# Moving token sums ahead of their splits, and two residual additions behind, in the last projection of a two-layer trunk

## The chip, the core and the metric

The kernel runs on one NeuronCore of a Trainium2 chip. The metric is the device time of one execution, in microseconds (us). Five engines work side by side, each through its own list of instructions in order, and wait for each other by semaphores: TensorE (PE in the profile; PEld is its weight load) multiplies matrices into banks of PSUM, VectorE (DVE) and ScalarE (ACT) do elementwise work, GpSimd (POOL) and SyncE (SP) here mostly issue DMA transfers.

## The reference

The model has two layers and a last norm. The second layer is multi-head latent attention; the change lies in its output projection, the last matrix product of the program:

```python
def mla_layer(x, cos, sin, norm_g, w_in, q_norm_g, w_q_b, kv_norm_g, w_kv_b, w_out):
    ...
    o = causal_mla_attention(q_nope, q_rope, k_nope, k_rope, v)
    y = o.reshape(B, S, MLA_WIDTH) * jax.nn.silu(z)
    return x + y @ w_out          # y: 512 x 2048, w_out: 2048 x 1024

def reference(...):
    ...
    return rmsnorm(x, final_norm)  # 512 x 1024, float32
```

`y` is 512 tokens by 2048 channels, `w_out` 2048 by 1024, `x` is the residual, all in float32.

## The kernel before

**Three matmuls for one.** A float32 operand is split into a high part and the rest: ScalarE writes `hi` (line 188 for tokens, 559 for weights), VectorE subtracts and writes `lo` (line 189, 560). `mm3` then multiplies hi by hi, lo by hi and hi by lo (lines 183, 184, 185) into the same bank. Each line of the profile with 183 to 185 is one of those three.

**Seven products for eight.** The projection is cut in two by tokens, by channels and by output columns, and is done by seven half-size products in the manner of Strassen, on sums of token blocks (`a11`, `a12`, `a21`, `a22`, all pieces of the tile `y`, stored with channels on the partitions) and on sums of weight blocks. VectorE makes the token sums (`combine_rows`, line 1055, two 128-channel rows at a time, 512 columns per instruction). `split_rows` cuts four rows at a time (1024 columns per instruction) into one of two token buffers, `slots[0]` and `slots[1]`, each with a `hi` and a `lo`. The weight sums are made by the DMA itself: SyncE loads a block (line 548), GpSimd issues a load that adds onto it (line 546). There are two such sets of weight tiles, `x_sum` (named `b_x`, four loads of 256 KB a strip) and `y_sum` (named `b_y`, two loads of 512 KB a strip).

**Strips and banks.** A product is `multiply(banks, strips, slot, start)`: two strips of weights of four rows each (`q` = 0, 1), and for each strip two token tiles (`t` = 0, 1) in two PSUM banks; four parts of 12 matmuls, 48 in all. A strip has a `hi` and a `lo` buffer from a ring of four (`WB = 4`), so there is room for two strips: strip `q` of a product can be split only when TensorE is done with strip `q` of the product before. With `start=False` the product adds onto what the banks hold. `gather` (line 610) is the addition of a bank to the residual `xs`, on VectorE, 512 columns; a product that goes on in that bank has to wait for it.

**What sets the order.** The tail is written in `products` and `finish` under a manual schedule: every engine does its share in the order in which it is written there. The first product runs inside the last heads of the attention; then follow

1. second: banks `both`, strips `t1` of `x_sum`, `slots[0]`
2. third: banks `last`, strips `p2` of `y_sum`, `slots[1]` (tokens `a12`)
3. fourth: banks `both`, strips `y1` of `y_sum`, `slots[0]` (tokens `n3 = s2 + a12`, written over `a12`)
4. fifth: banks `acc`, strips `t2` of `x_sum`, `slots[1]` (tokens `s2`)
5. sixth: banks `acc`, strips `y2` of `y_sum`, `slots[0]`
6. seventh, in `finish`, with the last norm and the stores.

Between the fourth and the fifth stand also `square` (ScalarE, line 1219: sums of squares of the residual for the last norm) and `total` (GpSimd).

Of the kernel before, what the change touches and what calls it, by code (L numbers as in the profile page):

```python
# [15 lines left out]
ALU = mybir.AluOpType  # L16
# [34 lines left out]
def trunk_kernel(  # L51
# [41 lines left out]
    def bank(dtype=F32):  # L93
        return ps.tile([P, 512], dtype, name="bank", tag="bank")
# [92 lines left out]
    def halves(src, hi, lo):  # L187
        act.activation(hi, src, AF.Copy)  # L188
        dve.tensor_tensor(lo, src, f32(hi), ALU.subtract)
# [51 lines left out]
    def start():  # L241
# [85 lines left out]
        for k in range(4):  # L327
            ready(0, k)
            products(0, k)
        w_lo(0, 4, 2)  # L330
        w_lo(1, 4, 2)
        ready(0, 4)
        products(0, 4)
        square(2)
        power(2)
        ready(0, 5)
        products(0, 5)
        ready(0, 6)
        scale(2)
# [194 lines left out]
    LEFT, RIGHT = slice(0, 512), slice(512, D)  # L534
# [35 lines left out]
    def quarters():  # L570

        return [
            [
                y[:, half * 8 + 2 * i : half * 8 + 2 * i + 2, t * 256 : (t + 1) * 256]
                for i in range(4)
            ]
            for t in range(2)
            for half in range(2)
        ]
# [21 lines left out]
    def multiply(banks, strips, slot, start, then=None):  # L601
        for q in range(2):
            for t in range(2):
                part(banks[t], strips[q], slot, q, t, start and q == 0, q == 1, not start)
                if then and q == 1:
                    then(t)

    def gather(t, c, b, op=ALU.add):

        dve.tensor_tensor(xs[:, t, c], xs[:, t, c], b, op)  # L610


    a11, a12, a21, a22 = quarters()

    slots = [tuple(v[:, :, s * 256 : (s + 1) * 256] for v in (h_hi, h_lo)) for s in range(2)]
# [7 lines left out]
    x_sum, y_sum = Summed(w_out, 2), Summed(w_out, 2)  # L623
# [7 lines left out]
    acc = [bank() for _ in range(2)]  # L631
# [399 lines left out]
    def values(h):  # L1031
# [17 lines left out]
    a11, a12, a21, a22 = (  # L1049
        y[:, half * 8 : half * 8 + 8, t * 256 : (t + 1) * 256] for t in range(2) for half in range(2)  # L1050
    )

    def combine_rows(out, a, b, op, k0, k1):
        for k in range(k0, k1, 2):
            dve.tensor_tensor(*(v[:, k : k + 2, :] for v in (out, a, b)), op)  # L1055

    def split_rows(src, slot, k0, k1):
        halves(*(v[:, k0:k1, :] for v in (src, *slot)))
    x_sum, y_sum = Summed(w_out2, 1), Summed(w_out2, 2)
# [38 lines left out]
    first_half, slots = {}, {}  # L1098
    for h in range(H):
        p, odd = divmod(h, 2)  # L1100
        g, t = divmod(h + 5, 4)
        if h == 12:
# [3 lines left out]
            acc = [bank() for _ in range(2)]  # L1106
# [47 lines left out]
    s3, s2 = a21, a11  # L1154
# [5 lines left out]
    def products():  # L1160

        combine_rows(s1, a21, a22, ALU.subtract, 6, 8)
        split_rows(s1, slots[0], 6, 8)
        x_sum.load(1, RIGHT, add=True, pieces=range(4))
        t1.append(x_sum.strip(1))
        x_sum.load(1, RIGHT, add=True, pieces=range(4, 8))
        multiply(both, t1, slots[0], True)
        split_rows(a12, slots[1], 0, 4)
        p2 = [y_sum.strip(0)]
        split_rows(a12, slots[1], 4, 8)  # L1170
        combine_rows(s3, a11, a21, ALU.subtract, 6, 8)
        combine_rows(s2, s1, a11, ALU.subtract, 6, 8)
        for t in range(2):
            gather(t, LEFT, acc[t])
        p2.append(y_sum.strip(1))
        y_sum.load(1, RIGHT)
        multiply(last, p2, slots[1], True)
        n3 = a12
        combine_rows(n3, s2, a12, ALU.add, 0, 4)
        split_rows(n3, slots[0], 0, 4)  # L1180
        combine_rows(n3, s2, a12, ALU.add, 4, 8)
        split_rows(n3, slots[0], 4, 8)
        for t in range(2):
            gather(2 + t, RIGHT, both[t])
        y1 = y_sum.strips()
        y_sum.load(0, RIGHT, add=True)
        multiply(both, y1, slots[0], False)
        split_rows(s2, slots[1], 0, 4)
        split_rows(s2, slots[1], 4, 8)
        for t in range(2):  # L1190
            gather(t, LEFT, last[t])
            square(t, LEFT)
            total(t)
        t2 = x_sum.strips()
        x_sum.load(1, LEFT, add=True)
        multiply(acc, t2, slots[1], False)
        split_rows(s3, slots[0], 0, 4)
        split_rows(s3, slots[0], 4, 8)
        for t in range(2):
            gather(t, RIGHT, both[t])  # L1200
        y2 = [y_sum.strip(0)]
        for t in range(2):
            gather(t, RIGHT, acc[t], ALU.subtract)
        y2.append(y_sum.strip(1))
        for t in range(2):
            square(t, RIGHT)
            power(t)
        multiply(acc, y2, slots[0], False)
        split_rows(a22, slots[1], 0, 4)
        split_rows(a22, slots[1], 4, 8)  # L1210
# [6 lines left out]
    def square(t, c):  # L1217
        r = sm.tile([P, 1], F32, name="ssq", tag="ssq8", bufs=12)
        act.activation(
            junk[:, : c.stop - c.start], xs[:, t, c], AF.Square, scale=D**-0.5, accum_out=r  # L1220
        )
        ssq[t].append(r)

    def total(t):

        r = sm.tile([P, 1], F32, name="total")
        pool.tensor_scalar(r, ssq[t][0], EPS, None, ALU.add)
        for q in ssq[t][1:]:
            pool.tensor_tensor(r, r, q, ALU.add)
        ssq[t] = [r]  # L1230

    def power(t):

        rs[t] = sm.tile([P, 1], F32, name="rs")
        pool.tensor_tensor(rs[t], ssq[t][1], ssq[t][0], ALU.add)
        pool.tensor_tensor(rs[t], rs[t], mhalf, ALU.pow)
# [92 lines left out]
```

## Time and profile before

| | us |
|---|---|
| median of three runs | 718.78 |
| lowest, highest | 718.22, 719.83 |
| the profiled execution, its own time | 719.61 |
| its span, first to last instruction | 717.8 |
| TensorE busy | 701.5 |
| VectorE busy | 444.5 |
| ScalarE busy | 347.2 |

The span is what the rows of the trace fill; the execution's own time is 1.81 us longer than its span. Times in rows count from the span's start. A row of the timeline gives start, duration, engine, line, operation, output and inputs with their sizes, a count where equal instructions follow each other, and in brackets the idle time before it with the instruction that the profile takes to have ended it. Where a row stands for several instructions, its duration covers all of them; consecutive ones overlap slightly, so that the pitch (start to start) is a little shorter than the duration of one.

### The profile page before, as it was taken

The numbers are of one execution on the slowest core, as the hardware profiler recorded it, in microseconds if no ns is written. First come the engines' busy times: TensorE is split into PE (matmuls) and PEld (weight loads), VectorE is DVE, ScalarE is ACT, GpSimd is POOL, SyncE is SP. The second block draws the span as 40 slices with busy tenths as digits, with TensorE's granted clock in tenths as the row PEclk, the third lists the DMA queues.
The fourth block names the chain that finished last, engine by engine and source line by source line (L and its number), as shares of the span: only waits on it lengthen the run. The fifth ranks groups of instructions, "written<-read, shape, count | busy, mean of one in ns | idle before, by whom it ended". The sixth has DMA issues, their size and how long they took to land.

```text
span 717.8 us, 10049 instructions
## 1 busy us (share of the span) xinstructions
PE 701.5 (98%) x3529; PEld 600.8 (84%) x3529; DVE 444.5 (62%) x866; ACT 347.2 (48%) x748; POOL 138.0 (19%) x182
## 2 busy tenths in 40 slices
PE   6999999999999999999999999999999999998996
PEld 6988888888888888799888888898899889986785
DVE  5963452562586897751644211686776787798775
ACT  6452332241343565554642324755575575655553
POOL 5000000000001341154600006221232131031621
PEclk9999999999999999999999999999999999999899
DMA  7342332333355997233432524113132265287843
GB/s 250 113 145 69 117 91 86 105 90 100 101 155 135 236 195 124 89 110 107 125 115 73 140 74 125 53 45 89 53 95 59 73 164 136 44 202 176 156 79 118
DMA packets 69475, 82.79 MB, mean 115 GB/s; under 512 B 12080, under 2 KB 45872, under 8 KB 69424
## 3 DMA queue, kind: packets, MB, share of 16 engines
q1 hardware_dynamic: 60384, 65.10, 30.2%
q0 software_dynamic: 8896, 16.78, 13.7%
q8 instruction: 28, 0.46, 0.3%
q10 hardware_dynamic: 144, 0.26, 0.1%
q14 instruction: 23, 0.19, 0.1%
HBM read 75.83 MB, written 2.10 MB: 109 GB/s over the span
## 4 chain that ended last, share of the span: by engine, by line
PE 93%; DVE 3%; issue 1%; ACT 1%; DMA 0%; POOL 0%; POOLq 0%; SPq 0%; DVEq 0%; ACTq 0%
PE bank L184 28%; PE bank L183 28%; PE bank L185 28%; PE bank L1022 2%; PE bank L301 2%; PE bank L986 1%; PE bank L985 1%; DVE w_lo L560 1%; DVE y L1055 1%; PE bank L226 1%; PE bank L1044 0%; PE bank L988 0%; DVE xs L610 0%; DMA xs<-in_x 0%; ACT a_hi L188 0%
## 5 line engine op out<-in xcount | busy, mean ns | idle before, releaser
L166 ACT ACTIVATE w_hi<-raw 128x512 fp32r<-128x512 f32 (+2 forms) x192 | 100.2, 576 | 134.3 <-PE bank L184 121.2
L167 DVE TENSOR_TENSOR w_lo<-raw,w_hi 128x512 fp32r<-128x512 f32 x124 | 81.6, 691 | 114.7 <-ACT w_hi L166 114.0
L183 PE MATMUL bank<-h_hi,w_hi 128*128 128x512 f32 x368 | 143.5, 390 | 0.0
L185 PE MATMUL bank<-h_lo,w_hi 128*128 128x512 f32 x368 | 143.3, 389 | 0.0
L184 PE MATMUL bank<-h_hi,w_lo 128*128 128x512 f32 x368 | 143.3, 389 | 0.0
L167 POOL TENSOR_TENSOR w_lo<-raw,w_hi 128x256 fp32r<-128x256 f32 (+2 forms) x68 | 61.3, 927 | 175.4 <-ACT w_hi L166 174.5
L185 PEld LDWEIGHTS bank<-h_lo,w_hi 128*128 128x128 f32 x368 | 69.1, 188 | 14.4
L184 PEld LDWEIGHTS bank<-h_hi,w_lo 128*128 128x128 f32 x368 | 69.1, 188 | 14.2
L183 PEld LDWEIGHTS bank<-h_hi,w_hi 128*128 128x128 f32 x368 | 69.1, 188 | 14.2
L183 PE MATMUL bank<-w_hi,h_hi 128*128 128x512 f32 (+1 forms) x176 | 64.6, 367 | 0.0
L184 PE MATMUL bank<-w_hi,h_lo 128*128 128x512 f32 (+1 forms) x176 | 64.2, 364 | 0.0
L185 PE MATMUL bank<-w_lo,h_hi 128*128 128x512 f32 (+1 forms) x176 | 64.1, 364 | 0.0
L183 PE MATMUL bank<-w_hi,a_hi 128*128 128x512 f32 (+1 forms) x116 | 45.9, 395 | 2.5 <-ACT w_hi L559 2.5
L185 PE MATMUL bank<-w_lo,a_hi 128*128 128x512 f32 (+1 forms) x116 | 45.6, 393 | 0.5 <-DVE w_lo L560 0.5
L184 PE MATMUL bank<-w_hi,a_lo 128*128 128x512 f32 (+1 forms) x116 | 45.6, 393 | 0.0
L183 PE MATMUL bank<-latT_hi,w_hi 128*128 128x512 f32 x104 | 42.4, 408 | 0.0
L184 PE MATMUL bank<-latT_hi,w_lo 128*128 128x512 f32 x104 | 40.6, 391 | 0.0
L185 PE MATMUL bank<-latT_lo,w_hi 128*128 128x512 f32 x104 | 40.6, 390 | 0.0
L559 ACT ACTIVATE w_hi<-b_x 128x512 fp32r<-128x512 f32 (+1 forms) x40 | 29.8, 796 | 20.9 <-PE bank L184 10.3
L560 DVE TENSOR_TENSOR w_lo<-b_x,w_hi 128x512 fp32r<-128x512 f32 (+1 forms) x40 | 34.0, 900 | 9.4 <-ACT w_hi L559 9.3
L183 PEld LDWEIGHTS bank<-w_hi,h_hi 128*128 128x128 f32 x176 | 33.1, 188 | 4.4
L185 PEld LDWEIGHTS bank<-w_lo,h_hi 128*128 128x128 f32 x176 | 33.1, 188 | 4.4
(204 smaller groups left out, 1404.8 us busy)
## 6 DMA issues: line engine op xcount, KB each, us to landing
raw<-in_pool_w_in SPq DMA_DIRECT2D x64, 256.0 KB, 3.0
raw<-in_mla_w_in SPq DMA_DIRECT2D x32, 256.0 KB, 3.1
b_x<-in_pool_w_out POOLq DMA_DIRECT2D x12, 512.0 KB, 7.6
b_x<-in_mla_w_out POOLq DMA_DIRECT2D x24, 256.0 KB, 6.5
raw<-in_mla_w_q_b SPq DMA_DIRECT2D x36, 128.0 KB, 2.3
raw<-in_pool_w_group SPq DMA_DIRECT2D x16, 256.0 KB, 2.7
q_r<-stack SPq DMA_DIRECT2D x64, 64.0 KB, 2.0
raw<-in_mla_w_kv_b SPq DMA_DIRECT2D x16, 256.0 KB, 3.0
```

What stands on the lines that cost most here:

```text
L166: act.activation(hi, raw, AF.Copy)
L167: ins = eng.tensor_tensor(lo, raw, f32(hi), ALU.subtract)
L183: pe.matmul(o, a[0], b[0], start=start, stop=False, skip_group_check=more)
L184: pe.matmul(o, a[1], b[0], start=False, stop=False, skip_group_check=more)
L185: pe.matmul(o, a[0], b[1], start=False, stop=stop, skip_group_check=more)
L226: pe.transpose(pt[:, i * P : (i + 1) * P], xn[:, k * P : (k + 1) * P], ident)
L301: pe.matmul(first[i][:, c], w0.views[0][a][:, k, i * P : (i + 1) * P], (h_hi, h_lo)[b][:, k, c], start=k == 0 and n == 0, stop=k == KD - 1 ...
L559: act.activation(hv[:, k, :], raw, AF.Copy)
L560: eng.tensor_tensor(lv[:, k, :], raw, f32(hv[:, k, :]), ALU.subtract)
L985: pe.matmul(o, q_r[h // 4][:, h % 4, c], k_a[:, :n], start=True, stop=False)
L986: pe.matmul(o, q_r[h // 4][:, h % 4, c], k_b[:, :n], start=False, stop=False)
L1022: pe.transpose(b[:, n : n + P], pm[:, OFF[i] + j * P : OFF[i] + (j + 1) * P], ident)
```

## The change

Only the order of lines in `products` changes. Nothing is added or taken out, no size and no queue is changed.

- The second strip of the third product (`p2`) is split before the last rows of `s3` and `s2` are summed, and no longer after two `gather`s.
- All four sums of `n3` (rows 0 to 8) are made in one go, before the first split of `n3`. Before, rows 4 to 8 were summed after rows 0 to 4 had been split.
- The two `gather`s of `both` and the first strip of `y1` come before the second half of `n3` is split.
- The two `gather`s of the left half from `acc` go from ahead of the third product's second strip to behind the fourth product's second strip.

```diff
         split_rows(a12, slots[1], 0, 4)
         p2 = [y_sum.strip(0)]
         split_rows(a12, slots[1], 4, 8)
+        p2.append(y_sum.strip(1))
         combine_rows(s3, a11, a21, ALU.subtract, 6, 8)
         combine_rows(s2, s1, a11, ALU.subtract, 6, 8)
-        for t in range(2):
-            gather(t, LEFT, acc[t])
-        p2.append(y_sum.strip(1))
         y_sum.load(1, RIGHT)
         multiply(last, p2, slots[1], True)
         n3 = a12
-        combine_rows(n3, s2, a12, ALU.add, 0, 4)
+        combine_rows(n3, s2, a12, ALU.add, 0, 8)
         split_rows(n3, slots[0], 0, 4)
-        combine_rows(n3, s2, a12, ALU.add, 4, 8)
-        split_rows(n3, slots[0], 4, 8)
         for t in range(2):
             gather(2 + t, RIGHT, both[t])
-        y1 = y_sum.strips()
+        y1 = [y_sum.strip(0)]
+        split_rows(n3, slots[0], 4, 8)
+        y1.append(y_sum.strip(1))
+        for t in range(2):
+            gather(t, LEFT, acc[t])
         y_sum.load(0, RIGHT, add=True)
         multiply(both, y1, slots[0], False)
```

On VectorE, from the last split of `a12` (the first row) to the splits of `s2` for the fifth product, the order was this (`a_lo` is the `lo` of a token split, `w_lo` that of a strip, `y<-y` and `y<-s_5950,y` are token sums, `xs<-xs,bank` a `gather`):

```order
L189 TENSOR_TENSOR a_lo<-y,a_hi 128x1024
L1055 TENSOR_TENSOR y<-y 128x2x256
L1055 TENSOR_TENSOR y<-s_5950,y 128x2x256
L610 TENSOR_TENSOR xs<-xs,bank 128x512 x2
L560 TENSOR_TENSOR w_lo<-b_y,w_hi 128x1024 x2
L1055 TENSOR_TENSOR y<-y 128x2x256 x2
L189 TENSOR_TENSOR a_lo<-y,a_hi 128x1024
L1055 TENSOR_TENSOR y<-y 128x2x256 x2
L189 TENSOR_TENSOR a_lo<-y,a_hi 128x1024
L610 TENSOR_TENSOR xs<-xs,bank 128x512 x2
L560 TENSOR_TENSOR w_lo<-b_y,w_hi 128x1024 x4
L189 TENSOR_TENSOR a_lo<-y,a_hi 128x1024 x2
```

The same stretch of VectorE with the change:

```order
L189 TENSOR_TENSOR a_lo<-y,a_hi 128x1024
L560 TENSOR_TENSOR w_lo<-b_y,w_hi 128x1024 x2
L1055 TENSOR_TENSOR y<-y 128x2x256
L1055 TENSOR_TENSOR y<-s_5950,y 128x2x256
L1055 TENSOR_TENSOR y<-y 128x2x256 x4
L189 TENSOR_TENSOR a_lo<-y,a_hi 128x1024
L610 TENSOR_TENSOR xs<-xs,bank 128x512 x2
L560 TENSOR_TENSOR w_lo<-b_y,w_hi 128x1024 x2
L189 TENSOR_TENSOR a_lo<-y,a_hi 128x1024
L560 TENSOR_TENSOR w_lo<-b_y,w_hi 128x1024 x2
L610 TENSOR_TENSOR xs<-xs,bank 128x512 x2
L189 TENSOR_TENSOR a_lo<-y,a_hi 128x1024 x2
```

The same 20 instructions stand there: the first `w_lo` pair has gone ahead of six sums in a row, one `w_lo` pair now stands between the two `a_lo` of `n3`, and the second pair of `gather`s is the one from `acc`.

On ScalarE, at the same place, the difference between the two orders (- before, + with the change; the first two rows are the third product's, the last two the fifth's tokens and the squares):

```order
 L188 ACTIVATE a_hi<-y 128x1024
 L559 ACTIVATE w_hi<-b_y 128x1024 x2
-L188 ACTIVATE a_hi<-y 128x1024 x2
-L559 ACTIVATE w_hi<-b_y 128x1024 x4
+L188 ACTIVATE a_hi<-y 128x1024
+L559 ACTIVATE w_hi<-b_y 128x1024 x2
+L188 ACTIVATE a_hi<-y 128x1024
+L559 ACTIVATE w_hi<-b_y 128x1024 x2
 L188 ACTIVATE a_hi<-y 128x1024 x2
 L1219 ACTIVATE junk,ssq<-xs 128x512 x2
```

The first strip of `y1` now stands ahead of the second token split of `n3`. The order on TensorE, GpSimd and SyncE is unchanged; SyncE's and GpSimd's loads of `y_sum` still wait for the `w_lo` that reads the tile they write to.

## The prediction

> **What bounds the kernel now.** I read the page first, then who TensorE waited for in the last 118 us, then the rows there.
>
> ```profile
> PE 701.5 (98%) x3529; PEld 600.8 (84%) x3529; DVE 444.5 (62%) x866; ACT 347.2 (48%) x748; POOL 138.0 (19%) x182
> PE 93%; DVE 3%; issue 1%; ACT 1%; DMA 0%; POOL 0%; POOLq 0%; SPq 0%; DVEq 0%; ACTq 0%
> ```
>
> TensorE is busy for 98% of the span and carries 93% of the chain that ended last. Earlier work on another engine pays only where TensorE stands still. The waits of TensorE from 600 us to the end are two:
>
> ```profile
> PE bank L183 <- ACT w_hi L559: 2.5, 1, 2.5
> PE bank L185 <- DVE w_lo L560: 0.5, 1, 0.5
> ```
>
> Both lie at one place, the start of the fourth product (timeline of TensorE; "..." leaves out regular rows):
>
> ```profile
> 655.21 0.39 PE L183 MATMUL bank<-w_hi,a_hi 128*128 128x512 f32 x1
> ...
> 660.42 0.39 PE L185 MATMUL bank<-w_lo,a_hi 128*128 128x512 f32 x1
> 663.29 0.69 PE L183 MATMUL bank<-w_hi,a_hi 128*128 128x512 f32 x1 [2.48 <-ACT w_hi L559]
> ...
> 664.94 0.80 PE L185 MATMUL bank<-w_lo,a_hi 128*128 128x512 f32 x1 [0.52 <-DVE w_lo L560]
> ...
> 677.97 0.39 PE L183 MATMUL bank<-w_hi,a_hi 128*128 128x512 f32 x1
> ```
>
> From 655.21 to 660.42 there are 23 steps, 0.227 us each: that is the pitch. The fourth product could have begun at 660.42 + 0.23 = 660.65 and, with 48 matmuls, the fifth at 660.65 + 10.90 = 671.55. The fifth began at 677.97. **The place costs 6.42 us**, more than the 3.0 us of waits. The rest is the clock (PEclk, the column after POOL, in half-microsecond windows):
>
> ```profile
> 662.50:663.00 0.50, 0.00 (x0) 0.00 (x0) 0.50 (x2) 0.50 (x1) 0.00 (x0) 1.00 0.00 0
> 663.50:664.00 0.50, 0.50 (x2) 0.19 (x1) 0.50 (x2) 0.50 (x1) 0.00 (x0) 0.50 0.00 0
> 669.50:670.00 0.50, 0.50 (x3) 0.40 (x2) 0.50 (x1) 0.00 (x0) 0.50 (x1) 0.50 1.10 201
> 670.50:671.00 0.50, 0.50 (x4) 0.41 (x3) 0.50 (x2) 0.00 (x0) 0.00 (x0) 1.00 0.92 139
> ```
>
> Just after the wait TensorE runs at half clock, for nearly 7 us. Split of the 6.42: the third matmul started at 664.94 instead of 661.10, that is 3.84 for the waits; the other 2.6 are half clock.
>
> Why the wait? VectorE and ScalarE hold the rows:
>
> ```profile
> 649.37 1.22 DVE L189 TENSOR_TENSOR a_lo<-y,a_hi 128x1024 fp32r<-128x1024 f32 x1
> 650.50 0.68 DVE L1055 TENSOR_TENSOR y<-y 128x512 f32<-128x512 f32 x1
> 651.22 0.69 DVE L1055 TENSOR_TENSOR y<-s,y 128x512 f32<-128x512 f32 x1
> 651.83 1.28 DVE L610 TENSOR_TENSOR xs<-xs,bank 128x512 f32<-128x512 f32 x2
> 653.02 2.35 DVE L560 TENSOR_TENSOR w_lo<-b_y,w_hi 128x1024 fp32r<-128x1024 f32 x2
> 655.29 1.29 DVE L1055 TENSOR_TENSOR y<-y 128x512 f32<-128x512 f32 x2
> 657.71 1.23 DVE L189 TENSOR_TENSOR a_lo<-y,a_hi 128x1024 fp32r<-128x1024 f32 x1 [1.13 <-ACT a_hi L188]
> ...
> 661.32 1.23 DVE L189 TENSOR_TENSOR a_lo<-y,a_hi 128x1024 fp32r<-128x1024 f32 x1 [1.18 <-ACT a_hi L188]
> 662.47 1.28 DVE L610 TENSOR_TENSOR xs<-xs,bank 128x512 f32<-128x512 f32 x2
> 663.66 4.62 DVE L560 TENSOR_TENSOR w_lo<-b_y,w_hi 128x1024 fp32r<-128x1024 f32 x4
> 668.20 2.35 DVE L189 TENSOR_TENSOR a_lo<-y,a_hi 128x1024 fp32r<-128x1024 f32 x2
> 670.47 1.28 DVE L610 TENSOR_TENSOR xs<-xs,bank 128x512 f32<-128x512 f32 x2
> 673.22 2.50 DVE L560 TENSOR_TENSOR w_lo<-b_x,w_hi 128x512 fp32r<-128x512 f32 x4 [1.47 <-ACT w_hi L559]
> ...
> 686.87 0.68 DVE L610 TENSOR_TENSOR xs<-xs,bank 128x512 f32<-128x512 f32 x1
> ```
>
> ```profile
> 649.74 2.01 ACT L559 ACTIVATE w_hi<-b_y 128x1024 fp32r<-128x1024 f32 x2 [0.98 <-PE bank L184]
> 656.62 1.06 ACT L188 ACTIVATE a_hi<-y 128x1024 fp32r<-128x1024 f32 x1 [4.86 <-DVE y L1055]
> 660.23 1.06 ACT L188 ACTIVATE a_hi<-y 128x1024 fp32r<-128x1024 f32 x1 [2.56 <-DVE y L1055]
> 661.20 3.88 ACT L559 ACTIVATE w_hi<-b_y 128x1024 fp32r<-128x1024 f32 x4
> 671.19 0.63 ACT L1219 ACTIVATE junk<-xs 128x512 f32<-128x512 f32 x1 [4.22 <-DVE xs L610]
> ...
> 672.57 2.18 ACT L559 ACTIVATE w_hi<-b_x 128x512 fp32r<-128x512 f32 x4
> ```
>
> The token sum, `hi`, `lo` go to and fro twice, in a line: sum, a_hi (656.62), a_lo (657.71), sum, a_hi (660.23), a_lo (661.32), then the additions out of `both` (662.47), then the strip's w_lo (663.66). The first addition is done at 662.47 + 0.68 = 663.15; the first matmul, which goes on in that bank, starts 0.14 us later (the profile names w_hi, whose first piece was done at 662.26, so I put this wait down to the addition). The third starts when w_lo is done, 663.66 + 1.22 = 664.88. Neither engine is short of time: ScalarE sat idle for 4.86 and 2.56 us, VectorE for 1.13 and 1.18. The order makes the wait.
>
> **The change, worked out.** No instruction is added or removed, and I use pitches of the rows above: 1.14 us for 1024 columns on VectorE (1.22 until done), 0.60 for 512 (0.68 until done), 0.95 for 1024 on ScalarE (1.06 until done). Up to 650.5 nothing changes.
>
> VectorE: the third product's second strip w_lo waits for w_hi (649.74 + 1.06) and runs 650.83 to 653.1; s3 and s2 take 1.33 as before, to 654.4; four sums to 656.8, the second of them done at 655.7. ScalarE then does a_hi of rows 0 to 4 from 655.75 to 656.8, the two first w_hi of y1 from 656.7 (first done 657.8, second 658.7), a_hi of rows 4 to 8 to 659.7, and the second strip's w_hi when the third product lets go of its buffer, about 660.6, to 662.6. VectorE: a_lo from 656.85 to 658.0; the additions out of `both` to 659.2, the first done at 658.7; w_lo of the first strip done at 660.4 and 661.6; a_lo of rows 4 to 8 done at 662.7; w_lo of the second strip done at 663.8 and 665.0.
>
> Fourth product, starting at 660.65: its first matmul needs the addition (658.7) and w_hi (657.8), 1.9 us to spare; its third, at 661.10, w_lo (660.4), **0.7 to spare**, the least; its ninth, at 662.47, the second w_lo (661.6); its 25th to 27th, from 666.1, the second strip and rows 4 to 8 (663.8). The wait is gone, and with it the half clock: −6.42.
>
> Loads: SyncE loads y1's tiles when p2's w_lo has read them.
>
> ```profile
> 649.48 0.37 SPq L548 DMA_DIRECT2D b_y<-in_mla_w_out  x1
> ...
> 655.40 0.37 SPq L548 DMA_DIRECT2D b_y<-in_mla_w_out  x1
> ```
>
> ```profile
> DMA to landing us min/median/max: 6.8/6.9/6.9
> ```
>
> ```profile
> DMA to landing us min/median/max: 4.1/6.2/10.4
> ```
>
> (The first landing line is that of the two loads of the first strip, the second of all 12 loads of `b_y`.) The first strip's second tile lands at 649.48 + 6.9 = 656.4 and is wanted at 657.7, as nothing before it moves. The second strip's loads go out about 2.2 us earlier, at 652.1 and 653.2; even with 10.4 us they are there by 663.6, its w_lo about 665.9, wanted at 666.5. GpSimd's adding loads for the sixth product wait for y1's w_lo, which comes 4.5 us earlier for the first, about 3 for the last; strips of the sixth are wanted at 677.0 and 682.4. All hidden.
>
> **What is late next.** The two additions from `acc` cost 1.2 us of VectorE; they were hidden in front and now stand in front of the fifth product. VectorE goes on: additions 664.9 to 666.1, a_lo of s2 to 668.4, additions from `last` to 669.6. Then as in the rows: w_hi of t2 starts 2.10 after those additions start (670.47 to 672.57; squares lie between), w_lo 0.65 after w_hi. So w_hi starts at 670.5, w_lo at 671.15. The fifth product wants its first w_hi at 671.55 (done about 671.1) and its first w_lo at 672.0 (done 671.83): 0.2 us to spare where before it had over 4; then w_lo comes every 0.60 and is wanted every 0.68. The sixth starts in `acc` at 682.45 and wants the addition that was done at 687.55 before:
>
> ```profile
> 688.85 0.39 PE L183 MATMUL bank<-w_hi,a_hi 128*128 128x512 f32 x1
> ```
>
> There it had 1.3 to spare. Now w_lo of t2's second strip runs 673.6 to 676.0, right behind the first; two a_lo to 678.3, two additions to 679.5, two w_lo to 681.8, the addition done at 682.5: about 0.1 late. Nothing is late behind it, since TensorE's buffers pace the strips again. I take 0.2 for both places, bounds 0 (my times err early) and 1.3 (VectorE runs 1.1 us later than I have it).
>
> **Sum:** −6.42 + 0.2 = −6.2. The profiled execution, 719.61 (span 717.8), would take 713.4; it was 0.83 above the median of the runs. On the median, 718.78 − 6.2 = **712.6**.
>
> **Rivals.**
>
> *The half clock isn't all won back* (714.9). Whether the clock falls depends on how the wait lies against whatever watches TensorE; in the timed executions before it may have stayed up, and then the wait cost only 3.84: 718.78 − 3.84 = 714.9. For it: the timed runs differ by 1.6 us among themselves and their median is 0.83 under the profiled one. Against: the one execution that is shown has it. [...]
>
> *The wait moves to the fifth product* (713.8). If ScalarE's first split waits for all four sums instead of two, it starts at 656.85, and everything behind is 1.1 us later: 0.4 at the fourth product's third matmul, 0.9 more at the fifth and sixth, 1.3 in all beside 0.1 of mine. 718.78 − 6.42 + 1.4 = 713.8. Against: before, ScalarE went on 0.04 us after the second sum was done.
>
> *Slower* (720). The fifth product inherits the whole wait: if VectorE comes to it 3 us later than worked out (slowed by GpSimd, which now issues its loads beside y1's splits), TensorE idles 2.8 us there, the clock halves as it did (2.6), and the sixth, whose addition hangs on the same engine, waits 2 more: 7.4 − 6.42 = +1.0. It decides from about 2.5 us. Against: before, VectorE's four w_lo (663.66 to 668.28) ran while GpSimd issued the same kind of loads, at no slower pitch than elsewhere (4.62 for four, 2.35 for two):
>
> ```profile
> 666.56 3.64 POOL L546 DMA_DIRECT2D b_y<-in_mla_w_out  x3 [0.16 <-issue]
> ```
>
> *The split isn't freed at all* (718.8): if y1's first w_hi had to wait for the third product's end, it would start at 660.6, as before. The ring of four buffers speaks against it: the buffer is that of p2's first strip, and the last matmul that reads it is 24 steps before 660.42, at 655.0.
>
> **How the numbers follow.** Forecast 0.72, half clock not won back 0.13, moved to the fifth product 0.10, no effect 0.03, slower 0.02. Differences under 0.2% (1.4 us) can't be told from none here. The first three are faster by more than that: 0.95; same 0.03; slower 0.02. The likeliest is 712.6. The range goes from 711.8 (all 6.42 and 0.5 for how medians of three scatter) to 715.0, which takes in the two faster rivals.
>
> **What would show it.** TensorE's row after the third product has no idle time; PEclk is 1.00 through 660 to 672; VectorE's first addition out of `both` starts near 658 and its w_lo of y1 near 659.2; the fifth product starts near 671.6 and the sixth near 682.6; the span is near 711.6. A wait of TensorE over 0.5 us anywhere from 655 on, a half clock there, or a split of `n3` after 656.5 would prove the working wrong; a trace with no wait but a time over 715 would prove the reading of the clock wrong.

## The result, and the profile after

| | before | after |
|---|---|---|
| median of four executions, us | 718.79 | 713.77 |
| lowest, highest | 718.22, 719.83 | 712.35, 714.51 |
| the profiled execution, its own time | 719.61 | 713.76 |
| its span | 717.8 | 712.0 |

The ratio is 0.9923, with a 95% interval of 0.991 to 0.9936: the kernel is 4.6 to 6.5 us faster. The forecast, 712.6, was 1.2 us too low; the range, 711.8 to 715.0, holds the time.

The page of the changed kernel, busy times and the chain of waits by engine:

```profile
PE 699.5 (98%) x3529; PEld 600.0 (84%) x3529; DVE 444.2 (62%) x866; ACT 347.0 (49%) x748; POOL 138.3 (19%) x182
PE 97%; DVE 1%; DMA 1%; POOL 0%; issue 0%; ACT 0%; POOLq 0%; SPq 0%; ACTq 0%
```

VectorE's share of the chain fell from 3% to 1%, TensorE's rose from 93% to 97%. The waits of TensorE over the whole execution are now these. The first two lines lie in the first 10 us, the third at 302 us, where the second layer begins; the two of the last projection are gone:

```profile
PE bank L271 <- DVE xn L264: 3.0, 2, 1.6
PE bank L127 <- POOL ident masks.py:199: 1.9, 1, 1.9
PE bank L226 <- DVE xn L218: 0.6, 1, 0.6
```

The timeline of TensorE around the starts of the fourth, fifth and sixth product ("..." leaves out regular rows):

```profile
660.89 0.39 PE L185 MATMUL bank<-w_lo,a_hi 128*128 128x512 f32 x1
661.12 0.39 PE L183 MATMUL bank<-w_hi,a_hi 128*128 128x512 f32 x1
...
672.00 0.39 PE L183 MATMUL bank<-w_hi,a_hi 128*128 128x512 f32 x1
...
682.65 0.39 PE L185 MATMUL bank<-w_lo,a_hi 128*128 128x512 f32 x1
682.93 0.47 PE L183 MATMUL bank<-w_hi,a_hi 128*128 128x512 f32 x1
683.24 0.40 PE L184 MATMUL bank<-w_hi,a_lo 128*128 128x512 f32 x1
```

The fourth product follows the third at the pitch, 0.23 us after its last matmul. The fifth starts 10.88 us later, which is 48 pitches of 0.2267 (the prediction's 10.90 rounds the pitch up): nothing is lost. Only the sixth is late: 0.05 us at its first matmul (0.28 after the one before) and 0.08 at the next, about 0.13 in all. The windows of the same stretch (first column after the length is PE, the third from the end PEclk):

```profile
655.00:670.00 15.00, 15.00 (x68) 12.43 (x67) 15.00 (x18) 8.30 (x9) 4.80 (x4) 1.00 0.73 180
```

TensorE is busy throughout at full clock, where before it ran at 0.50 for nearly 7 us. VectorE and ScalarE there:

```profile
651.30 2.36 DVE L560 TENSOR_TENSOR w_lo<-b_y,w_hi 128x1024 fp32r<-128x1024 f32 x2 [0.26 <-ACT w_hi L559]
...
654.91 2.49 DVE L1055 TENSOR_TENSOR y<-y 128x512 f32<-128x512 f32 x4
657.32 1.23 DVE L189 TENSOR_TENSOR a_lo<-y,a_hi 128x1024 fp32r<-128x1024 f32 x1
658.46 1.28 DVE L610 TENSOR_TENSOR xs<-xs,bank 128x512 f32<-128x512 f32 x2
659.66 2.35 DVE L560 TENSOR_TENSOR w_lo<-b_y,w_hi 128x1024 fp32r<-128x1024 f32 x2
...
665.34 1.27 DVE L610 TENSOR_TENSOR xs<-xs,bank 128x512 f32<-128x512 f32 x2
...
671.55 4.91 DVE L560 TENSOR_TENSOR w_lo<-b_x,w_hi 128x512 fp32r<-128x512 f32 x8 [1.47 <-ACT w_hi L559]
```

```profile
656.23 1.06 ACT L188 ACTIVATE a_hi<-y 128x1024 fp32r<-128x1024 f32 x1 [4.00 <-DVE y L1055]
657.19 1.99 ACT L559 ACTIVATE w_hi<-b_y 128x1024 fp32r<-128x1024 f32 x2
```

VectorE's six sums stand in one row, and ScalarE's first split of `n3` starts at 656.23, just after the second of the four sums is done (654.91 + 0.60 + 0.68 = 656.19): it waits for two sums, not four. The first `w_lo` of `y1` is done at 659.66 + 1.22 = 660.88; the third matmul of the fourth product wants it at 661.57.

**Where the time went, by these two traces.** From the end of the third product to the start of the fifth, 6.44 us were won (677.97 − 660.65 = 17.32 before, 10.88 now); the sixth gives 0.13 back. The third product itself ended 0.47 us later than before, at 661.12 against 660.65, and this is not the change: nearly all of the delay is there at the end of the program's first 26 us, which it doesn't touch (below, under "The start kept busy"). 6.44 − 0.47 − 0.13 = 5.84; the two times differ by 5.85.

### The profile page after: what moved, and what is told of

Read it like the earlier page. It is cut to its first block, busy times and chain, and to the rows that moved or that the text cites. A ratio compares the mean times of both kernels' runs of the same rounds, so it can differ in the third digit from the quotient of the medians.

```text
span 712.0 us, 10047 instructions
## 1 busy us (share of the span) xinstructions
PE 699.5 (98%) x3529; PEld 600.0 (84%) x3529; DVE 444.2 (62%) x866; ACT 347.0 (49%) x748; POOL 138.3 (19%) x182
## 4 chain that ended last, share of the span: by engine, by line
PE 97%; DVE 1%; DMA 1%; POOL 0%; issue 0%; ACT 0%; POOLq 0%; SPq 0%; ACTq 0%
PE bank L184 29%; PE bank L183 29%; PE bank L185 29%; PE bank L1022 2%; PE bank L301 2%; PE bank L986 1%; PE bank L985 1%; PE bank L226 1%; PE bank L271 1%; DMA xs<-in_x 1%; PE bank L988 0%; PE bank L1044 0%; PE bank L751 0%; DVE xn L218 0%; ACT junk L1219 0%
## 5 line engine op out<-in xcount | busy, mean ns | idle before, releaser
L184 PEld LDWEIGHTS bank<-h_hi,w_lo 128*128 128x128 f32 x368 | 69.1, 188 | 14.2
```

The lines of the kernel that those rows point to most:

```text
L184: pe.matmul(o, a[1], b[0], start=False, stop=False, skip_group_check=more)
```

## The experiments

The theory is the prediction's: the order of sums and splits on two engines that were not short of time made the wait; the wait made the half clock; with the wait gone the fifth and sixth product follow with next to nothing to spare. Rivals: the half clock has a cause of its own; one of the four moved pieces does everything; the half clock was a chance of the one profiled execution.

"Loss" is how late the fifth product starts against the regular pitch from the end of the third, 10.88 us for 48 matmuls (6.44 in the prediction's trace, which the prediction, with 10.90, put at 6.42). What the sixth adds is named beside it. Time differences are taken to the median of the kernel before that ran on the same chip beside it: 719.41 for the first four, 718.56 for the next four.

### The sums alone

The kernel before, with one of the change's edits: all sums of `n3` ahead of its splits.

```diff
-        combine_rows(n3, s2, a12, ALU.add, 0, 4)
+        combine_rows(n3, s2, a12, ALU.add, 0, 8)
         split_rows(n3, slots[0], 0, 4)
-        combine_rows(n3, s2, a12, ALU.add, 4, 8)
         split_rows(n3, slots[0], 4, 8)
```

> One part alone: the kernel before with the four sums of n3 in one go, all else as it was. Theory (the to and fro between sum, hi and lo makes the wait, and the half clock follows from the wait): VectorE's first addition out of `both` ends about 660.7 and the first w_lo of y1 about 662.5, wanted at 661.1, so TensorE loses about 1.4 us at the fourth product, and a wait that short leaves the clock at 1.00: about 1.4 above the changed kernel, 715.2. If the clock halves all the same, 717.8. Rival (the strip's place behind both token splits is what counts, the sums' place is not): 718.8, no change.

Measured 714.93, ratio 0.9932 (0.9917 to 0.9947), that is 4.5 us less. In the trace the loss is 1.63 us, one wait, and the clock stays at 1.00 behind it. TensorE's row:

```profile
661.25 0.50 PE L185 MATMUL bank<-w_lo,a_hi 128*128 128x512 f32 x1 [0.94 <-DVE w_lo L560]
```

VectorE's rows of the same kernel:

```profile
656.37 2.49 DVE L189 TENSOR_TENSOR a_lo<-y,a_hi 128x1024 fp32r<-128x1024 f32 x2
658.78 1.28 DVE L610 TENSOR_TENSOR xs<-xs,bank 128x512 f32<-128x512 f32 x2
659.98 4.63 DVE L560 TENSOR_TENSOR w_lo<-b_y,w_hi 128x1024 fp32r<-128x1024 f32 x4
```

Both `a_lo` now run back to back, one row in place of two with a sum and idle time between them. This one edit brings most of the change, and the half clock goes with it.

### The strips alone

The kernel before, with the additions out of `both` and the first strip of `y1` moved ahead of the second sums and splits.

```diff
         split_rows(n3, slots[0], 0, 4)
-        combine_rows(n3, s2, a12, ALU.add, 4, 8)
-        split_rows(n3, slots[0], 4, 8)
         for t in range(2):
             gather(2 + t, RIGHT, both[t])
-        y1 = y_sum.strips()
+        y1 = [y_sum.strip(0)]
+        combine_rows(n3, s2, a12, ALU.add, 4, 8)
+        split_rows(n3, slots[0], 4, 8)
+        y1.append(y_sum.strip(1))
```

> One part alone: the kernel before with the additions out of `both` and the first strip of y1 ahead of the second sums and second split of n3; sums not joined, additions from `acc` not moved. Theory: the first w_lo ends about 661.3 (wanted 661.1), the second strip's about 667.0 (wanted 666.5), together 0.6 at the fourth product; then the strip for the fifth comes about 0.9 late: 1.5 in all, clock at 1.00, 715.3. Rival (only joined sums help): 718.8.

Measured 715.53, ratio 0.9946 (0.993 to 0.9963): 3.9 us less. The loss is about 1.9 us: 0.3 at the third matmul, 0.4 at the second strip, and 1.2 at the fifth product, where the later second half now arrives; 0.1 more comes at the sixth. The row of the fifth:

```profile
671.80 0.50 PE L183 MATMUL bank<-w_hi,a_hi 128*128 128x512 f32 x1 [0.74 <-ACT w_hi L559]
```

The to-and-fro is still there, only behind the first strip, and its cost has moved to the fifth product, partly.

### The additions alone

The kernel before, with the two additions from `acc` moved behind `y1`; the third product's second strip comes 1.2 us earlier by that.

```diff
-        for t in range(2):
-            gather(t, LEFT, acc[t])
         p2.append(y_sum.strip(1))
...
         y1 = y_sum.strips()
+        for t in range(2):
+            gather(t, LEFT, acc[t])
```

> One part alone: the kernel before with the two additions from `acc` moved behind y1, and with them the third product's second strip ahead of the last sums of s3 and s2; sums and strips of n3 as before. Theory: all of the chain comes 1.2 us earlier, the first addition out of `both` ends about 662.2 and the first w_lo about 663.9, so TensorE still waits 1.5 and then 1.3 us, 2.8 in all: 716.6 with the clock at 1.00, 719.2 with a half clock of 2.6. Rival (moving the additions is the whole gain): 713.8.

Measured 717.31, ratio 0.9964 (0.9948 to 0.998): 2.1 us less. The loss in the trace is 2.77 us, both waits are still there, the first shorter by 1.19 us, and the clock doesn't fall. TensorE's rows, then the windows:

```profile
661.63 0.47 PE L183 MATMUL bank<-w_hi,a_hi 128*128 128x512 f32 x1 [1.29 <-ACT w_hi L559]
...
663.27 0.50 PE L185 MATMUL bank<-w_lo,a_hi 128*128 128x512 f32 x1 [0.94 <-DVE w_lo L560]
```

```profile
665.00:670.00 5.00, 5.00 (x24) 4.14 (x23) 5.00 (x6) 0.31 (x1) 3.54 (x3) 1.00 0.93 150
```

By the trace 3.7 us should have come, and the median shows 2.1. The five executions fall in two groups, 715.54 and 715.69 against 717.31, 717.56 and 717.72. Traced once more:

> The kernel with only the additions from `acc` moved, again: its waits of 1.29 and 0.94 us left the clock up in the first trace, but its times fell in two groups, 715.6 and 717.5. Theory (stretches lie anywhere): the same waits; half clock behind them in this trace or not, 717.5 with it, 715.6 without, unless the start makes the difference. Rival (waits this short never lower the clock): 1.00 there again.

This execution took 715.57, loss 2.77, clock 1.00 behind the waits. So both traces are of the quicker group, and they give the trace's 3.7. What the slower group has isn't shown. The mean granted clock of its executions (0.990, 0.994, 0.990, against 0.994 and 0.998 of the quicker) says that two of them spent 14 us at half clock (2 × 0.010 × 716), against 3 us in the execution with 0.998. In the profiled executions of the kernel before and of the changed one 3.2 and 3.6 us of half clock lie at the very end of the span, where TensorE has done its work; that much accounts for the 3 us and leaves some 10 of the 14. This would fit a clock that falls at these shorter waits in some executions, but it was not seen.

### The wait filled

The kernel before, in its own order, with ten matmuls of 512 columns between the third and the fourth product. Nobody reads their bank. TensorE is busy while it would wait; everything else is as before. (The added lines make the line numbers of `mm3` 184 to 186 here.)

```diff
 WARM = 17
+FILL = 10
...
         multiply(last, p2, slots[1], True)
+        spare = bank()
+        for _ in range(FILL):
+            pe.matmul(spare, identr, slots[1][0][:, 0:2, :], start=True, stop=True)
         n3 = a12
```

> The kernel before, with ten matmuls of 512 columns that nobody reads put between the third and the fourth product, 2.3 us, so that TensorE is busy while it waits; order of all other engines unchanged. Theory (the half clock comes from TensorE standing idle): the waits' 3.84 us stay, the clock stays at 1.00 through 660 to 672 and the other 2.6 us go: 716.2. Rival (the half clock has another cause, such as a wait too short to matter or the load of the other engines): it halves all the same, 718.8 or up to 0.5 more.

Measured 717.33, ratio 0.9963 (0.995 to 0.9976): 2.1 us less, with more work for TensorE and the same lateness of the other engines. TensorE's rows, then the windows:

```profile
659.55 2.50 PE L1181 MATMUL bank<-a_hi,identr 128*128 128x512 f32 x10
662.19 0.47 PE L184 MATMUL bank<-w_hi,a_hi 128*128 128x512 f32 x1
...
663.83 0.50 PE L186 MATMUL bank<-w_lo,a_hi 128*128 128x512 f32 x1 [0.94 <-DVE w_lo L561]
```

```profile
662.00:664.00 2.00, 0.92 (x4) 0.47 (x4) 2.00 (x4) 2.00 (x4) 0.00 (x0) 1.00 0.00 0
664.00:666.00 2.00, 2.00 (x9) 1.62 (x10) 2.00 (x3) 1.87 (x2) 1.77 (x2) 1.00 0.00 0
666.00:668.00 2.00, 2.00 (x10) 1.66 (x9) 2.00 (x3) 0.00 (x0) 2.00 (x3) 1.00 0.84 137
```

The fourth product's first matmul still starts 2.6 us after the third product's end, the second wait of 0.94 us is still there, and the loss is 3.98 (the fifth product starts at 674.41): the 3.84 of the waits and what the steps behind them add. But PEclk stays at 1.00. That separates the two parts of the 6.44: the half clock follows from TensorE's standing still, and not from the order of the other engines, which is the same here. It is one trace; the mean granted clocks of the five executions, 0.993 to 0.998 against 0.988 to 0.995 in the kernel before beside them, point the same way.

### The changed kernel again, and with the additions back in front

The changed kernel once more, beside the three variants of it that follow:

> The changed kernel itself again, for comparison on one chip with the next three. Both theories: 713.8, 5.0 to 6.3 under the kernel before, no wait of TensorE from 600 us on except under 0.1 us at the sixth product; what is left of the spread between executions lies in the first 20 us (half clock for one or two stretches of 3.4 us, 0.5 us apart between the two traces so far).

Measured 713.31 (712.26 to 714.29), ratio 0.9925 (0.9909 to 0.994). Then the changed kernel with the additions from `acc` back ahead of the third product's second strip:

```diff
-        p2.append(y_sum.strip(1))
         combine_rows(s3, a11, a21, ALU.subtract, 6, 8)
         combine_rows(s2, s1, a11, ALU.subtract, 6, 8)
+        for t in range(2):
+            gather(t, LEFT, acc[t])
+        p2.append(y_sum.strip(1))
...
         y1.append(y_sum.strip(1))
-        for t in range(2):
-            gather(t, LEFT, acc[t])
```

> The changed kernel with the two additions from `acc` put back where they were, ahead of the third product's second strip; the rest of the change stays. Theory (they are 1.2 us of VectorE ahead of the fourth product, which had 0.7 to spare): the first w_lo of y1 ends 0.5 us too late, TensorE loses 0.5 there and nothing later; 0.5 above the changed kernel. Rival (the additions are hidden in either place): no wait of TensorE at all, 0.0.

Measured 713.28 (712.4 to 714.04), the same. In its trace the fourth product's third matmul and the next are late by 0.33 us in all, and the sixth, late by 0.12 beside it, is not: 0.2 us net, which times that scatter by 2 us can't show. TensorE's rows:

```profile
660.14 0.39 PE L184 MATMUL bank<-w_hi,a_lo 128*128 128x512 f32 x1
660.58 0.50 PE L185 MATMUL bank<-w_lo,a_hi 128*128 128x512 f32 x1
660.92 0.39 PE L183 MATMUL bank<-w_hi,a_hi 128*128 128x512 f32 x1
```

Once the sums stand in one go and the first strip is early, moving the additions is worth almost nothing.

### The fifth product made late

The changed kernel, with the `lo` of rows 4 to 8 of `s2` computed twice: 1.14 us more for VectorE ahead of the fifth product, with the same result.

```diff
         split_rows(s2, slots[1], 4, 8)
+        hi, lo = (v[:, 4:8, :] for v in slots[1])
+        dve.tensor_tensor(lo, s2[:, 4:8, :], f32(hi), ALU.subtract)
```

> The changed kernel with one token split of s2 on VectorE done twice (1.14 us), between the fourth product's strips and the fifth's. Theory (the fifth product has 0.2 us to spare on VectorE): TensorE waits about 0.7 at the fifth product's first matmul and 0.2 at its third, 0.1 to 0.2 more at the sixth, clock at 1.00: 1.0 above the changed kernel. Rival (VectorE has room there, the time is hidden): 0.0, no wait.

Measured 714.36 (713.9 to 714.76), ratio 0.994 (0.9927 to 0.9953): 1.05 us over the changed kernel beside it. In the trace the fifth product loses 1.3 us up to its end. Its first row, and the waits of TensorE from 600 us on:

```profile
672.00 0.50 PE L183 MATMUL bank<-w_hi,a_hi 128*128 128x512 f32 x1 [0.68 <-ACT w_hi L559]
```

```profile
PE bank L183 <- ACT w_hi L559: 0.7, 1, 0.7
```

So nearly every tenth of a microsecond that VectorE is later here is one for the whole kernel: the fifth product has no cover left. (This traced execution also lost some 0.6 us far ahead of the edit: its third product ends 635.6 us after the last of the program's first products starts, and those of the changed kernel 634.9 and 635.0. That is not in the 1.3.)

### The start kept busy

The third product ended at 661.12 us in the changed kernel's profiled execution and at 659.5 in that of its repetition, the same program. The groups of TensorE's line 301, the first products of the program (minimum, median and maximum duration in ns, then the start of the first and of the last), first the one, then the other:

```profile
L301 PE MATMUL bank<-h_hi,w_hi x32: 280/283/582, 11.6 to 26.1; 128*128 128x256 f32 x32
```

```profile
L301 PE MATMUL bank<-h_hi,w_hi x32: 278/283/384, 10.2 to 24.6; 128*128 128x256 f32 x32
```

The whole difference, 1.5 us, is there when the last of these starts, at 26.1 and 24.6; from then on the two run alike. In the kernel before the same row ends at 25.7: 0.42 us earlier than the 26.1, of the 0.47. In this start TensorE waits several times (1.58 and 1.46 us ahead of the two token tiles' transposes in the first of the two), and behind the waits it ran at a recorded half clock in 6 of the 14 traces of this case. The windows of 8 to 16 us of the two:

```profile
8.00:16.00 8.00, 6.54 (x33) 5.97 (x31) 6.31 (x13) 6.21 (x15) 6.58 (x11) 0.57 0.87 285
```

```profile
8.00:16.00 8.00, 6.15 (x47) 5.59 (x48) 6.53 (x14) 6.87 (x16) 6.25 (x11) 1.00 0.88 290
```

33 matmuls in the one, at a mean clock of 0.57, and 47 in the other. Would unread work in TensorE's waits keep the clock up? The changed kernel, with 8 unread transposes ahead of the first token tile's and 8 ahead of the second's:

```diff
+        for _ in range(8):
+            pe.transpose(warm[:, :P], ident, ident)
         square(0)
         power(0)
         scale(0)
         turn(0)
+        for _ in range(8):
+            pe.transpose(warm[:, :P], ident, ident)
         square(1)
```

> The changed kernel with eight transposes that nobody reads after the first 17 at the start and eight between the first and the second token tile's transposes, where TensorE stood idle 1.6 and 1.5 us; the order elsewhere is unchanged. Theory (idling halves the clock there as it did at the fourth product): the clock stays at 1.00 from 7 to 16 us, and the time falls by 1 to 2 us, 712.3, with less spread. Rival (transposes don't count as activity, or the half clock at the start has another cause): half clock at the start as before, 713.8, or up to 1 more if they hold up the real ones.

Measured 713.5 (711.85 to 713.79), ratio 0.9921 (0.9904 to 0.9937): no gain. In its trace the clock still falls, for 3.4 us. TensorE's rows, then the windows:

```profile
6.98 1.09 PE L271 MATMUL bank<-ident,xn 128*128 128x128 f32 x8 [0.55 <-DVE xn L264]
7.91 1.04 PE L320 MATMUL bank<-ident 128*128 128x128 f32 x8
10.22 1.09 PE L271 MATMUL bank<-ident,xn 128*128 128x128 f32 x8 [1.27 <-DVE xn L264]
```

```profile
12.00:13.00 1.00, 0.98 (x5) 0.93 (x5) 1.00 (x4) 1.00 (x4) 1.00 (x2) 0.52 0.44 160
14.00:15.00 1.00, 1.00 (x6) 1.00 (x6) 0.61 (x2) 1.00 (x3) 0.92 (x3) 0.50 0.95 320
```

Whether the 1.27 us that stayed idle were enough to bring it down, or transposes of 128 columns don't keep it up as the ten matmuls of 512 columns did, is open. The count of idle time in the next section speaks for the second: 1.51 us of it stood here ahead of the fall, while up to 1.71 us left the clock up in other starts.

### The kernel before, traced three times more

A trace is one execution, and the prediction took 2.6 us for the half clock from one. Three more traces of the same kernel, with no edit:

> The kernel before, unchanged, for another trace. Theory (the waits at the fourth product are the same in every execution, 3.84 us at its third matmul; the clock is judged in stretches of 3.4 us that lie anywhere against them, so that the half clock there lasts two stretches, one or none): the same two waits, half clock of 6.8, 3.4 or 0 us, loss up to the fifth product 6.4, about 5 or 3.84. Rival (the half clock is the same each time): 6.8 us and 6.4 again.

> As the trace before it: the same waits, and 6.8, 3.4 or 0 us of half clock behind them. Rival: 6.8 each time.

> As the two before it: the same waits, and 6.8, 3.4 or 0 us of half clock behind them; over three traces not all the same. Rival: 6.8 each time.

| execution | time, us | half clock recorded in the first 20 us | half clock at the fourth product | loss | loss beyond 3.84 of waits | idle in the 3.41 us ahead of the fall |
|---|---|---|---|---|---|---|
| the prediction's | 719.61 | 3.4 | 6.8 | 6.44 | 2.6 | 2.48 |
| first | 717.92 | 3.4 | 3.4 | 5.59 | 1.8 | 1.77 |
| second | 718.19 | 0 | 6.8 | 6.13 | 2.3 | 1.96 |
| third | 718.99 | 0 | 6.8 | 6.79 | 3.0 | 2.63 |

The first wait is 2.48 us every time, and the clock falls every time, but not at the same point. The rows and windows of the first of the three:

```profile
662.45 0.47 PE L183 MATMUL bank<-w_hi,a_hi 128*128 128x512 f32 x1 [2.48 <-ACT w_hi L559]
...
664.09 0.50 PE L185 MATMUL bank<-w_lo,a_hi 128*128 128x512 f32 x1 [0.94 <-DVE w_lo L560]
```

```profile
660.00:665.00 5.00, 1.61 (x6) 1.08 (x7) 4.52 (x5) 5.00 (x6) 0.67 (x1) 1.00 0.00 0
665.00:670.00 5.00, 5.00 (x17) 3.92 (x16) 5.00 (x6) 1.13 (x2) 4.19 (x4) 0.66 0.80 120
```

and of the second:

```profile
660.00:665.00 5.00, 2.43 (x5) 1.54 (x6) 4.84 (x6) 5.00 (x7) 0.99 (x1) 0.66 0.00 0
665.00:670.00 5.00, 5.00 (x16) 3.94 (x16) 5.00 (x6) 0.80 (x1) 3.87 (x4) 0.66 0.85 136
```

In the first the clock is still 1.00 through both waits and falls at 665, for one stretch of 3.4 us; in the second it falls within the first wait and stays at 0.50 for two. The place cost 5.6 to 6.8 us, 6.2 in the mean of the four.

The half clock lasts 3.4 us or 6.8, and by the windows it begins at 663.4, 665.0, 661.6 and 663.2 us, in the order of the table: 0.1 us behind the end of the first wait, 2.6 behind it, 0.5 ahead of it and 0.9 behind it. A wait of 2.48 us, with 0.5 to 0.9 us more behind it, brought the clock down in four traces of four. Waits of 1.29 and 0.94 us, with two matmuls between them, did it in neither of two.

**Idle time in one stretch.** The recorded clock of the prediction's trace changes at 11.43, 14.84, 663.38 and 670.20 us, which are 3.41, 648.54 and 6.82 us apart: 1, 190 and 2 times 3.413. In the first of the three new traces it changes at 9.66, 13.08, 665.02 and 668.44: 1, 191 and 1 times that apart. So the span of a trace can be cut into stretches of that length, with borders where its clock changes. At the fourth product the clock fell behind stretches in which TensorE was idle for 1.77 us or more (last column). It stayed up behind a stretch with 1.64, the one before the fall in the first of the three traces, and behind those of the other kernels: 0.97 and 1.26 for the additions alone, where a border of stretches divides the two waits, about 1.6 and 0.6 in their second trace (with the border taken from the change of pace at about 14.2 us, below), 1.08 with the wait filled, 0.94 for the sums alone. In the start it fell behind 1.78 to 2.19 us in five traces and stayed up behind 1.71 or less, with one exception, the start with unread transposes, where it fell behind 1.51. So the fall went here, but for that one, with the idle time in one stretch and not with the length of one wait alone: in the first of the three the border divided the 2.48 us, 1.64 to 0.84, and the clock stayed up until the stretch with the second wait was over. What sets the borders, no run shows. The additions alone have 2.2 us of waits within 3 us: in an execution where one stretch takes in both, this count would have the clock fall, which no trace shows. The recorded half clock ended behind a stretch with at most 0.4 us of idle time and went on behind those with 0.5 to 1.1; in the three traces with 6.8 us, the second wait lay in the first stretch of half clock. (Idle times are the profile's, in which the ends of matmuls are modelled.)

**A half clock that the profile doesn't record.** The records of the clock begin 4.6 us into the span in the prediction's trace and 5.2 us in that of the changed kernel, and ahead of the first the column shows 1.00. Two windows of the second trace of the additions alone, in which it shows 1.00 from 3 to 22 us:

```profile
12.50:13.00 0.50, 0.50 (x4) 0.50 (x4) 0.50 (x2) 0.48 (x2) 0.50 (x2) 1.00 0.63 193
15.00:15.50 0.50, 0.50 (x7) 0.50 (x6) 0.50 (x1) 0.50 (x3) 0.36 (x1) 1.00 0.19 48
```

The first has four matmuls of 256 columns, as the same half microsecond has at a recorded 0.50 in the prediction's trace, where two take 0.43 us by their starts (12.39 to 12.82); the second has seven, and at a recorded 1.00 two take 0.24 us there (14.91 to 15.15). The pace changes at about 14.2 us. So a 0 in the table's third column, and a high mean granted clock, don't exclude half speed at the very start.

## Why the prediction was right, and where it was off

- **The bound.** Right. TensorE alone sets the end, and only the place where it stood still paid: its waits there went from 3.0 us to none, and the 6.44 us of that place account for the difference of the two profiled executions, with the 0.47 and 0.13 named above.
- **The order makes the wait.** Right, and shown part by part: each of three parts alone shortens the same line, to a loss of 1.63 (sums), 1.9 (strips) and 2.77 us (additions) from 6.44. They don't add up: the sums alone bring 4.5 of the 5 us by the times. Not every part that was moved matters.
- **The wait makes the half clock.** Right, and shown by the filled wait. The rival that it is not all won back (714.9) falls as a cause: in all four traces of the kernel before the clock falls, in none of the changed kernel's two does it fall at that place. What that rival feared of the single trace was real, though: the 2.6 us is one draw out of 1.8 to 3.0. And how the wait lay showed in the time of the fall: 2.6 us behind the wait where a border of stretches divided its 2.48 us, 1.64 to 0.84, and from 0.5 us ahead of its end to 0.9 behind it in the other three.
- **ScalarE waits for two sums.** Right (0.04 us behind the second), so the rival by which it waits for four (713.8) falls, although its time is the one measured: its mechanism, 0.4 late at the fourth product and 0.9 at the fifth and sixth, is not in the trace. A time alone would have confirmed it.
- **What is late next.** Right to a tenth: 0.69 us to spare at the third matmul of the fourth product (predicted 0.7), 0.21 at the fifth (`w_lo` done at 671.55 + 0.69 = 672.24, wanted at 672.45; predicted 0.2), the sixth late by 0.13 (predicted 0.1). That the fifth has no cover is shown by the 1.05 us (1.3 in the trace) that 1.14 us of work cost there. The rival that was slower than before had its place right, but would have needed 2.5 us there.
- **The additions.** Moving them was worth 0.2 us by the traces (0.33 against 0.12), below what the times tell.
- **The loads.** Right: no wait for a load stands behind the third product, and GpSimd's four loads for the sixth, issued beside `y1`'s splits, slow nothing (`w_lo` keeps 2.35 us for two).
- **The number.** For the profiled execution 713.4 was predicted and 713.76 measured; the difference is the third product's later end, 0.47, less small change. On the median it was 712.6 against 713.77, and here one step failed: *"On the median, 718.78 − 6.2"*. It takes the loss of one trace off the median of other executions, and holds all else for constant. The runs show that neither holds. The place is a term with a spread, 5.6 to 6.8 us in four traces; their mean of 6.2, less 0.13, makes 6.1, while the medians differ by 5.0 and 5.25, and the means of all executions by 5.5 (28 of before, 718.9; 10 of after, 713.4; a scatter of 0.9 in each makes that 5.5 uncertain by some 0.7). And the start is a term of its own, up to 1.5 us, which the prediction did not have. The executions of the changed kernel show it in two groups: 712.26 to 712.87, with a mean granted clock of 0.997 or 0.998, and 713.75 to 714.51, with 0.992 or 0.993. The traced one of the first has no recorded half clock in the start, the traced one of the second has 6.8 us of it, and they differ by 1.5 us in both start and time. Four of ten lie in the first group, beside 712.6; the median falls into the second. That the other executions of the second group were also delayed in the start is inferred from their clock. The recorded half clock in the start went by the same count of idle time in a stretch (behind 1.78 to 2.19 us, not behind 1.71 or less), with one exception at 1.51; what sets where the stretches lie isn't settled, nor whether the 6.1 of the traces and the 5.5 of the times differ by more than chance.

No variant was measurably faster than the changed kernel: 713.28 and 713.5 stand beside 713.31.

## What to carry to other kernels

Where the engine that bounds a kernel stands still, look at the clock behind the wait as well as at the wait: here 3.8 us of waits cost 5.6 to 6.8. Add up the idle time around the wait too: at this place the clock fell behind 1.77 us or more within 3.41 us, not behind 1.64 or less, and the same wait of 2.48 us brought it down at once or only 2.6 us later. When two helper engines hand work to and fro while both have idle time, put the producer's steps in one go ahead of the consumer's, and work out whose cover that uses up: the next product had 0.2 us left, and 1.14 us more on VectorE cost 1.05. Take the size of a clock effect from several traces, and expect the median to move by less certain amounts than one trace promises.

## What the runs showed of the hardware that was not expected

- A wait of 2.48 us, with 0.5 to 0.9 us more close behind it, brought TensorE to half clock in four traces of four; the half clock lasted 3.4 us once and 6.8 us three times, though TensorE was busy from the second wait on (4.70 us of the 4.70 from 665.50 to 670.20 in the prediction's trace, at 0.50). Counted in stretches of 3.413 us, which the changes of the clock mark, it fell there behind 1.77 us of idle time or more, and not behind 1.64 or less.
- Ten unread matmuls of 512 columns in that wait (2.50 us) kept the clock at 1.00 and made the kernel 2.1 us faster, with more work done.
- In the first 20 us of the same work the profile records 0, 3.4 or 6.8 us of half clock: none in 8 of the 14 executions traced here, 3.4 in 5, 6.8 in 1. In one of the 8 the rows up to about 14.2 us went at half pace all the same, under a column of 1.00. In six traces of the kernel before and the changed one, the last of the first products starts between 24.5 and 26.1 us, and the third product of the last projection ends 634.9 to 635.0 us later in each: what differs between these executions ahead of the fourth product is made in the start. (One of the 14 had unread transposes added there.)
